# Last projection of a decoder trunk on one core: seven products for eight on 16 of its 22 feature blocks, set between the tiles of the projection before it

## The chip, the core and the metric

The program runs on one core of one Trainium2 chip. The core has a matrix engine (PE; its weight loads are shown apart as PEld), a vector engine (DVE), a scalar or activation engine (ACT), a general engine (POOL) and a queue engine that issues transfers (SP). Each engine takes its instructions in the order in which they were written and waits, where it must, for a signal of another engine or of a transfer. The metric is the device time of one execution in microseconds (us); lower is better. The time before is the median of three runs.

## The reference, cut to what matters

All arithmetic is in float32. The input `x` is (1, 512, 1024): 512 tokens of 1024 features, one layer. The part that the change touches is the channel mixer at the end and the last norm:

```
def conv_ffn(u, w_up, conv_w, conv_b, w_down):
    h = causal_dwconv(u @ w_up, conv_w, conv_b)
    a, v = h[..., :D_FF], h[..., D_FF:]
    return (jax.nn.silu(a) * v) @ w_down
...
        x = x + merged @ w_o[i]
        x = x + conv_ffn(rmsnorm(x, ln2_g[i]), ffn_w_up[i], ffn_conv_w[i], ffn_conv_b[i], ffn_w_down[i])
    return rmsnorm(x, final_g)
```

`D_FF` is 2816, that is 22 blocks of 128 features. `w_up` is 1024 x 5632, `w_down` is 2816 x 1024. The convolution has three taps along the tokens. Ahead of this stand a norm, a wide input projection, an attention, a pooling and a state-space branch, their gates, and the projection `w_o`.

## The kernel before

**Numbers.** Every matrix product is made of float32 operands split in a high and a low part (`wh`, `wl` for weights; `fh`, `fl` or `uh`, `ul` for the other side), each in a rounded format that the matrix engine takes. `mm3` (L230 is its matmul) adds three products, high by high, high by low and low by high, in one accumulator. The order matters below: the low part of the weights is only read in the last third of a group.

**Jobs.** The kernel is a list of jobs, each with a weight tile of 1 MB (some of 512 KB) and a body of matmuls. Before the body of job n is written, `prepare` writes three things: `low` of job n+1 (DVE: `wl = raw - wh`, L211), `cast` of job n+2 (ACT: `wh = raw`, L191, in two halves which are put off to the next two calls of `step`), and `fetch` of job n+3 (an SP transfer into `raw`, L179). There are two buffers for `raw`, three for `wh`, two for `wl`. `low` of job n+1 therefore waits until PE is done with job n-1, and `cast` until its transfer has landed. A job may have a `form` (its weights are a combination of loaded tiles, taken in place of `raw`), and a `then`, work on DVE that follows its `low`.

**Items.** Small work beside the matmuls (splitting a result, adding sums) is written as generators, in the list `running`. `step` is called once or twice a job; it writes the halves of a put-off `cast` first and then advances each running item by one piece.

**The up projection.** `up_jobs` makes 22 jobs. Jobs come in pairs: an even one holds two feature blocks of the half `a`, the odd one the same two blocks of `v`. Each has two chunks of 24 matmuls (128 x 128 by 512 columns). `up_evac` takes a chunk out of its accumulator `pu`: ACT scales it (L1162), DVE adds the two other taps (L1165 twice), then for `a` ACT applies silu (L1167), for `v` POOL multiplies with `a` (L1170). One `step` later the item `later` splits the block for the last projection (ACT L1177, DVE L1178).

**The last projection.** `down` and `blocks_of` follow after all up jobs. Output is kept in eight tiles `X1[tb, h]`, four token blocks by two halves of the 1024 columns, to which products are added. On the first `KS = 8` of the 22 blocks a two-by-two scheme with seven products instead of eight is used: blocks k and k+1 form the pair side, the column halves the other, and the token halves the third. A product is 24 matmuls (two token blocks i, four k blocks, three products of parts). The left sides are sums of the blocks (`sums_of`: four DVE operations of 256 columns, two ACT copies, two DVE differences for each pair of blocks), the right sides are combinations of quarters of `w_down` (`diff`, L333, 128 x 2048), where two quarters are loaded as `W`. The other 14 blocks are done plainly, by `blocks_of`, some in the same accumulators as two of the products. Because the scheme needs room, `put_x1` writes the eight `X1` tiles to DRAM after the fourth up job and `get_x1` brings them back after the last.

**The end.** `evac` of `blocks_of` adds the last accumulator, and for the second column half makes the final norm of that token block (`norm_late`) and sends it out. `tail=2` holds the last two jobs back and then runs them token block by token block.

**Buffers and queues.** Tiles of 128 x 512 come from one pool of `NBIG = 54`. `ypool`, tag `xs`, has two buffers of 128 x 4 x 512; before the change they hold `sh`, `sl` (parts of the sums) here. The order on PE, ACT, DVE and POOL is the order of writing; SP's order is set by a scheduler.

Of the kernel before, what the change touches and what calls it, by code (L numbers as in the profile page):

```python
# [10 lines left out]
F32 = mybir.dt.float32  # L11
# [5 lines left out]
P = 128  # L17
S = 512
# [10 lines left out]
SH = 16  # L29
DFF = 2816  # L30
KF = DFF // P
KS = 8
C_Q, C_K, C_V = 0, AW, 2 * AW
C_POOL = 3 * AW
C_Z = C_POOL + D
# [48 lines left out]
def trunk(ctx: ExitStack, tc, out, x, rel_bias, ln1_g, w_in, b_gate, w_a, pool_w, pool_scale, w_b,  # L84
# [26 lines left out]
    def MM(name):  # L111
        return psum.tile([P, S], F32, name=name, tag="mm")
# [978 lines left out]
    def get_x1():  # L1091
        back = upool.tile([P, KD, S], F32, name="x1b", tag="ul")
        for h in range(2):
            for tb in range(4):
                X1[tb, h] = back[:, 2 * tb + h, :]
                sp.dma_start(X1[tb, h], nxt["x1"][tb, h])

    def wo_jobs(pair, h):
        def evac(tb, ps):
            t = X1[tb, h]  # L1100
# [33 lines left out]


    ACTS = {}
    wide = []
    ff = {}

    def ff_cols():  # L1140
# [19 lines left out]
    def up_evac(m, ps):  # L1160
        t = HC[m] = T("hc")
        act.activation(t, ps, AF.Identity, bias=ff["c1"][:, ff["b"] + m:ff["b"] + m + 1], scale=fw(2, m))  # L1162
        for k in range(2):
            sh = 2 - k
            dve.scalar_tensor_tensor(t[:, sh:], ps[:, :S - sh], fw(k, m), t[:, sh:], OP.mult, OP.add)  # L1165
        if m < KF:
            act.activation(t, t, AF.Silu)  # L1167
            return
        a = HC[m - KF]
        pool.tensor_tensor(a, a, t, OP.mult)  # L1170

        def later():
            yield
            k = m - KF
            if k >= KS or k % 2:
                h, l = T("fh", F32R), T("fl", F32R)
                act.copy(h, a)  # L1177
                dve.tensor_sub(l, a, h.bitcast(F32))  # L1178
                ACTS[k] = (h, l)
                if k < KS:  # L1180
                    yield
                    for _ in sums_of(HC[k - 1], a, *(t[:, k // 2, :] for t in wide),
                                     lambda j, h, l: FS.__setitem__((j, k // 2), (h, l))):
                        yield
                return
            if k == 0:
                wide.extend(ypool.tile([P, 4, S], F32R, name=n, tag="xs") for n in ("sh", "sl"))
# [9 lines left out]
    def down():  # L1197

        n2 = KS // 2
        quarter = lambda two, h: w_down[:KS * P, h * S:(h + 1) * S].rearrange(
            "(k two p) c -> two p k c", two=2, p=P)[two]
        W, acc, rs, r3 = {}, {0: {}, 1: {}}, {}, {}

        def load_w():
            both = upool.tile([P, KD, S], F32, name="w3", tag="uh")
            for at in range(2):
                W[at] = both[:, 4 * at:4 * at + 4, :]
                sp.dma_start(W[at], quarter(at, 1))  # L1210
            get_x1()

        def product(ps, ws, parts, first, last):

            wh, wl = ws
            mm3(ps, lambda k: wh[:, k, :], lambda k: wl[:, k, :], lambda k: parts[k][0],
                lambda k: parts[k][1], range(n2), first, last, flip=True)

        def first_half(i):
            return [[t[:, i * P:(i + 1) * P] for t in FS[0, p]] for p in range(n2)]  # L1220

        def second_half(tb):
            return [[t[:, tb * P:(tb + 1) * P] for t in ACTS[2 * p + 1]] for p in range(n2)]

        def sums(j, i):
            return [[t[:, i * P:(i + 1) * P] for t in FS[j, p]] for p in range(n2)]

        def add(tb, h, what):
            dve.tensor_tensor(X1[tb, h], X1[tb, h], what, OP.add)

        def job(parts, use, form=None, ld=None):
            def body(ws):
                for i in range(2):
                    use(i, ws)
                    step()
            j = Job(parts, n2, S, body)
            j.form, j.load = form, ld
            return j


        def p2(i, ws):
            acc[0][i] = MM("pb")
            product(acc[0][i], ws, second_half(i), True, False)

        def p1(i, ws):
            ps = SM("p1")
            product(ps, ws, first_half(i), True, True)
            add(i, 0, ps)
            rs[i] = T("r1")
            act.copy(rs[i], ps)  # L1250
            if i:
                diff(W[0], W[1], W[0])

        def p5(i, ws):
            ps = SM("p5")
            product(ps, ws, sums(1, i), True, True)
            add(i, 1, ps)
            add(2 + i, 1, ps)

        def p7(i, ws):  # L1260
            ps = SM("p7")
            product(ps, ws, sums(3, i), True, True)
            r3[i] = T("r3")
            act.copy(r3[i], ps)

        def p6(i, ws):
            ps = SM("p6")
            product(ps, ws, sums(2, i), True, True)
            dve.tensor_tensor(rs[i], rs[i], ps, OP.add)
            dve.tensor_tensor(r3[i], r3[i], rs[i], OP.add)  # L1270

            def rest():
                yield
                add(2 + i, 0, r3[i])
                yield
                add(i, 1, rs[i])
                yield
                add(2 + i, 1, r3[i])
            running.append(rest())

        def p4(i, ws):
            product(acc[0][2 + i], ws, second_half(2 + i), False, True)
            add(2 + i, 0, acc[0][2 + i])
            running.append(early(2 + i))

        def p3(i, ws):
            acc[1][i] = SM("pb")
            product(acc[1][i], ws, sums(4, i), True, False)

        one = job([quarter(0, 0)], p1)  # L1290
        five = job([], p5, lambda: diff(one.raw, W[0], one.raw), lambda: None)
        def formed():
            diff(W[1], W[1], one.raw)
            return W[0]

        seven = job([], p7, formed, lambda: None)
        six = job([], p6, lambda: W[1], lambda: None)
        four = job([quarter(1, 0)], p4, lambda: diff(four.raw, four.raw, W[1]))
        plain = blocks_of(0, acc[0], (0, 1), (2, 3))

        yield Call(load_w)
        yield job([quarter(1, 0)], p2)
        yield next(plain)
        yield one
        yield five
        yield next(plain)
        yield seven
        yield next(plain)
        yield six
        yield from plain  # L1310
        yield four
        yield job([quarter(1, 1)], p3)
        yield from blocks_of(1, acc[1], (0, 1), ())

    def up_jobs():
        held = []
# [52 lines left out]
        yield  # L1369
        fin[tb] = norm_early(X1[tb, 0], fin["g"])  # L1370

    def blocks_of(h, acc, opened, keep):
# [12 lines left out]
        return jobs_b(lambda k0, k1: [wsrc(w_down, KS + k0, KS + k1, h * S, h * S + S)], S,  # L1385
                      lambda k, tb: ACTS[KS + k][0][:, tb * P:(tb + 1) * P],
                      lambda k, tb: ACTS[KS + k][1][:, tb * P:(tb + 1) * P], KF - KS, evac,
                      mk=(MM, SM)[h], tail=2 if h else 0, acc=acc, opened=opened, keep=keep)


    class Call:
# [3 lines left out]
    def program():  # L1395
# [34 lines left out]
        for pair in range(2):  # L1430
            for h in range(2):
                yield from wo_jobs(pair, h)
            if pair == 0:
                yield Call(ff_cols)
        for i, job in enumerate(up_jobs()):
# [220 lines left out]
```

## Time and profile before

| what | value |
|---|---|
| runs (us) | 1046.50, 1048.81, 1051.13; median 1048.81 |
| the profiled execution's own time | 1049.47 us |
| its span in the profile | 1047.4 us |
| granted PE clock over the span | 0.997 |
| matmuls | 5220 |
| up projection, full tiles | from about 696 to 925.5 us |
| last projection | from about 925.5 to 1040.5 us |
| what follows the last matmul | about 6.9 us |
| transfers over the span | 121.80 MB |

The span is what the profiler saw between the first and the last instruction; the execution's own time holds about 2 us more around it. Busy time of an engine is the sum of its instructions. "Idle before, releaser" says which signal ended an engine's wait. A matmul's record is longer than the distance to the next one, since they are pipelined; distances are read from the starts.

### The profile page before, as it was taken

To read this page: it belongs to the slowest core of one execution; us is meant where nothing else is said; L and a number is where in the kernel's file an instruction comes from. 1 tells how busy PE (TensorE), PEld (TensorE's weight loads), DVE (VectorE), ACT (ScalarE), POOL (GpSimd) and SP (SyncE) were. 2 spreads that over 40 slices of the span, in tenths; PEclk is the share of its full clock that TensorE was granted. 3 is DMA by queue.
4 is the path that set the end of the run, shared out by engine and by line. 5 is a ranking of instruction groups with operands and counts; after the bars stand their busy time and mean duration, and the time that the engine had idled before them with its cause. 6 is when DMAs were issued, how large, how long until landed. Compare 5 with 4: busy or idle time off the path is not lost.

```text
span 1047.4 us, 13090 instructions
## 1 busy us (share of the span) xinstructions
PE 1036.3 (99%) x5220; PEld 864.5 (83%) x5220; DVE 642.6 (61%) x865; ACT 467.6 (45%) x753; POOL 138.0 (13%) x118
## 2 busy tenths in 40 slices
PE   8999999999999999999999999999999999999997
PEld 8988877898888887787888888898888888878885
DVE  4563565774356647676658856766766566556645
ACT  5432555452474363557554324545444343433331
POOL 1680000000000001100143500001111111110110
PEclk9999999999999999999999999999999999999999
DMA  8445222127222363542252426643232322362322
GB/s 254 145 111 152 97 65 74 31 59 202 81 81 81 82 159 101 152 130 59 65 151 81 161 81 223 222 156 107 81 121 81 116 86 89 112 241 66 115 101 81
DMA packets 119787, 121.80 MB, mean 116 GB/s; under 512 B 5523, under 2 KB 101590, under 8 KB 119727
## 3 DMA queue, kind: packets, MB, share of 16 engines
q1 hardware_dynamic: 119135, 120.12, 37.1%
q8 instruction: 41, 0.67, 0.3%
q10 hardware_dynamic: 592, 0.86, 0.3%
q14 instruction: 19, 0.16, 0.0%
HBM read 115.07 MB, written 4.32 MB: 114 GB/s over the span
## 4 chain that ended last, share of the span: by engine, by line
PE 92%; DVE 3%; DMA 2%; ACT 2%; issue 0%; DVEq 0%; SPq 0%; ACTq 0%
PE pa L230 35%; PE pu L230 22%; PE pb L230 13%; PE pqk L230 9%; PE pa L1508 2%; PE p L230 2%; DVE wl L211 2%; PE ps L656 1%; PE po L695 1%; PE pt L683 1%; DMA raw<-in_ffn_w_up_dram 1%; PE ppw L230 1%; ACT wh L191 1%; PE py L955 1%; DMA raw<-in_w_o_dram 1%; PE pyo L961 1%
## 5 line engine op out<-in xcount | busy, mean ns | idle before, releaser
L211 DVE TENSOR_TENSOR wl<-raw,wh 128x2048 fp32r<-128x2048 f32 (+3 forms) x95 | 218.5, 2301 | 77.7 <-ACT wh L191 40.3
L191 ACT CAST wh<-raw 128x1024 fp32r<-128x1024 f32 (+3 forms) x188 | 189.6, 1026 | 67.4 <-DVE raw L333 21.1
L230 PE MATMUL pa<-uh,wh 128*128 128x512 f32 x384 | 98.7, 399 | 0.0
L1165 DVE SCALAR_TENSOR_TENSOR hc<-pu,fcol,hc 128x510 f32<-128x510 f32 x88 | 65.9, 748 | 50.8 <-ACT hc L1162 49.2
L230 PE MATMUL pa<-uh,wl 128*128 128x512 f32 x384 | 95.0, 389 | 0.0
L230 PE MATMUL pa<-ul,wh 128*128 128x512 f32 x384 | 94.9, 389 | 0.0
L230 PEld LDWEIGHTS pa<-ul,wh 128*128 128x128 f32 x384 | 72.1, 188 | 15.2
L230 PEld LDWEIGHTS pa<-uh,wl 128*128 128x128 f32 x384 | 72.0, 188 | 15.2 <-DVE wl L211 0.3
L230 PE MATMUL pu<-uh,wh 128*128 128x512 f32 (+1 forms) x352 | 83.7, 380 | 0.2 <-ACT uh L448 0.2
L230 PE MATMUL pu<-ul,wh 128*128 128x512 f32 (+1 forms) x352 | 83.5, 379 | 0.0
L230 PE MATMUL pu<-uh,wl 128*128 128x512 f32 (+1 forms) x352 | 83.5, 379 | 0.0
L230 PEld LDWEIGHTS pa<-uh,wh 128*128 128x128 f32 x384 | 70.2, 188 | 15.3 <-issue 1.0
L230 PEld LDWEIGHTS pu<-uh,wh 128*128 128x128 f32 x352 | 64.1, 188 | 12.8 <-ACT uh L448 0.4
L230 PEld LDWEIGHTS pu<-ul,wh 128*128 128x128 f32 x352 | 64.2, 188 | 12.5
L230 PEld LDWEIGHTS pu<-uh,wl 128*128 128x128 f32 x352 | 64.2, 188 | 12.5
L1162 ACT ACTIVATE hc<-pu,fcol,fcol 128x512 f32<-128x512 f32 x40 | 31.2, 780 | 75.5 <-PE pu L230 75.3
L1170 POOL TENSOR_TENSOR hc<-hc 128x512 f32<-128x512 f32 x22 | 31.5, 1432 | 223.6 <-DVE hc L1165 169.4
L934 POOL TENSOR_TENSOR xd<-xc,dec 128x512 f32<-128x512 f32 x6 | 6.4, 1065 | 360.1 <-DVE xc L925 334.5
L677 ACT ACTIVATE sb<-sb,nm 128x128 f32<-128x128 f32 (+1 forms) x72 | 30.1, 419 | 24.1 <-DVE nm L674 17.2
L1050 ACT ACTIVATE sg<-pa,col 128x512 f32<-128x512 f32 x24 | 16.5, 687 | 50.7 <-PE pa L230 50.6
L230 PE MATMUL pqk<-uh,wh 128*128 128x512 f32 x144 | 36.9, 394 | 0.0
L230 PE MATMUL pqk<-ul,wh 128*128 128x512 f32 x144 | 36.3, 389 | 0.0
(348 smaller groups left out, 1751.7 us busy)
## 6 DMA issues: line engine op xcount, KB each, us to landing
raw<-in_w_in_dram SPq DMA_DIRECT2D x25, 1024.0 KB
raw<-in_ffn_w_up_dram SPq DMA_DIRECT2D x22, 1024.0 KB
raw<-in_w_in_dram SPq DMA_DIRECT2D x20, 512.0 KB
raw<-in_ffn_w_down_dram SPq DMA_DIRECT2D x10, 1024.0 KB
raw<-in_w_o_dram SPq DMA_DIRECT2D x8, 1024.0 KB
raw<-in_w_b_dram SPq DMA_DIRECT2D x4, 1024.0 KB
al<-ad SPq DMA_DIRECT2D x16, 256.0 KB
raw<-in_w_c_dram SPq DMA_DIRECT2D x4, 1024.0 KB
```

The lines of the kernel that those rows point to most:

```text
L191: act.copy(job.high[:, :, o], job.raw[:, :, o])
L211: (eng or dve).tensor_tensor(l[:, :, o], job.raw[:, :, o], h[:, :, o].bitcast(F32), OP.subtract)
L230: pe.matmul(ps, l, r, start=first and n == 0, stop=last and n == total - 1)
L656: pe.matmul(pss[i][:, o:o + w * P], q[r, n * P:(n + 1) * P], k[r, kb * P:(kb + w) * P], start=True, stop=True)
L677: act.activation(sb[:, off:off + w * P], sb[:, off:off + w * P], AF.Exp, bias=nm[:, n, h:h + 1], accum_out=ls[:, n, h:h + 1])
L683: pe.transpose(pt[:, o:o + P], sb[:, o:o + P], eye)
L695: pe.matmul(po[DH * hh:DH * hh + DH, n * P:(n + 1) * P], V[g, kb + i][:, (2 * c + hh) * DH:(2 * c + hh + 1) * DH], probs[2 * c + hh, nb][: ...
L1050: act.activation(s, ps, AF.Sigmoid, bias=col[:, o:o + 1])
L1162: act.activation(t, ps, AF.Identity, bias=ff["c1"][:, ff["b"] + m:ff["b"] + m + 1], scale=fw(2, m))
L1165: dve.scalar_tensor_tensor(t[:, sh:], ps[:, :S - sh], fw(k, m), t[:, sh:], OP.mult, OP.add)
L1170: pool.tensor_tensor(a, a, t, OP.mult)
L1508: pe.matmul(first[2 * n + j][:, lo:hi], a[:, k, j * P:(j + 1) * P], b[:, k, lo:hi], start=a is wh and b is uh and k == 0, stop=a is wl and ...
```

## The change

`KS` goes from 8 to 16, in two groups of eight blocks. `down_group(base)` writes the seven products of a group as jobs of their own, and `program` sets them between the up jobs: the table `AT` says after which up job each product stands (22 stands for "after the first plain job of the last projection"). Six blocks are left for the plain scheme (`down_jobs`). No product shares an accumulator with plain blocks any more: every product goes through an accumulator `pd`, and its result is added to the `X1` tiles on DVE, or kept in a tile `r1`, `r2`, `r5`, `r7` by ACT and added later. The seven additions of a group's last steps are written one per step. `X1` stays on chip, and `put_x1` and `get_x1` are gone; the `xs` buffers now hold the two quarters `W` of a group. In `later` the four DVE sums are made in the same step as the high part of the odd block, one step sooner than before.

The order of jobs is then: up 0 to 9, three, up 10, seven, up 11, one, up 12, five, up 13, six, up 14, two, up 15, four (A22), up 16, up 17, three', seven', up 18, one', up 19, five', up 20, six', up 21, two', first plain job, four', the other plain jobs. (A prime marks the second group; three is the product of the fourth sum with `W[1]`, four the one of `A22`.)

```
-KS = 8
+KS = 16
...
-    def put_x1():
-        nxt["x1"] = dram.tile([4, 2, P, S], F32, name="x1d")
-        for tb, h in X1:
-            sp.dma_start(nxt["x1"][tb, h], X1[tb, h])
...
             if k >= KS or k % 2:
                 h, l = T("fh", F32R), T("fl", F32R)
                 act.copy(h, a)
+                it = iter(())
+                if k < KS:
+                    it = sums_of(HC[k - 1], a, T("sah", F32R), T("sal", F32R),
+                                 lambda j, h, l: FS.__setitem__((j, k // 2), (h, l)))
+                    next(it)
                 dve.tensor_sub(l, a, h.bitcast(F32))
                 ACTS[k] = (h, l)
-                if k < KS:
+                yield
+                for _ in it:
                     yield
...
+        def load():
+            for two in range(2):
+                W.append(ypool.tile([P, 4, S], F32, name="w3", tag="xs"))
+                sp.dma_start(W[two], quarter(two, 1))
...
+        def p1(i, ps):
+            keep(r1, "r1")(i, ps)
             add(i, 0, ps)
...
+        def p5(i, ps):
+            keep(r5, "r5")(i, ps)
+            dve.tensor_tensor(r2[i], r2[i], ps, OP.add)
+
+        def p6(i, ps):
+            dve.tensor_tensor(r1[i], r1[i], ps, OP.add)
 
             def rest():
                 yield
+                dve.tensor_tensor(r7[i], r7[i], r1[i], OP.add)
+                for tb, h, r in ((i, 1, r1), (2 + i, 0, r7), (i, 1, r2), (2 + i, 1, r7), (2 + i, 1, r5)):
+                    yield
+                    add(tb, h, r[i])
             running.append(rest())
...
+        def then1():
+            diff(W[0], W[0], one.raw)
+            dve.tensor_tensor(W[1], W[1], one.raw, OP.add)
+
+        one = job("A11", quarter(0, 0), None, p1)
+        two = job("A12", quarter(1, 0), None, lambda i, ps: add(i, 0, ps))
+        three = job(4, None, lambda: W[1], keep(r2, "r2"))
+        three.then = lambda: diff(W[1], W[1], W[0])
+        one.then = then1
+        two.then = lambda: diff(two.raw, two.raw, W[1])
+        return load, [[three], [job(3, None, lambda: W[1], keep(r7, "r7"))], [one],
+                      [job(1, None, lambda: W[0], p5)], [job(2, None, lambda: W[1], p6)],
+                      [two], [job("A22", None, lambda: two.raw, lambda i, ps: add(2 + i, 0, ps))]]
...
         for i, job in enumerate(up_jobs()):
             yield job
-            if i == 3:
-                yield Call(put_x1)
+            for load, ats in zip(loads, AT):
+                if i == ats[0] - 3:
+                    yield Call(load)
+            yield from between.get(i, ())
         yield Call(lambda: fin.setdefault("g", grow(final_g)))
-        yield Call(finish)
-        yield from down()
+        plain = down_jobs(0)
+        yield next(plain)
+        yield from between.get(2 * (KF // 2), ())
+        yield from plain
+        yield from down_jobs(1)
...
+AT = ((9, 10, 11, 12, 13, 14, 15), (17, 17, 18, 19, 20, 21, 22))
```

More of the change, by code (lines that the diff above doesn't have):

```diff
@@ L1136, in trunk @@
     ACTS = {}
-    wide = []
     ff = {}
@@ L1195, in trunk, with down_group @@
     FS = {}
-    def down():
-        n2 = KS // 2
-        quarter = lambda two, h: w_down[:KS * P, h * S:(h + 1) * S].rearrange(
+    def down_group(base):
+        quarter = lambda two, h: w_down[base * P:(base + 8) * P, h * S:(h + 1) * S].rearrange(
             "(k two p) c -> two p k c", two=2, p=P)[two]
[L1204 to L1226, printed above, removed]
@@ new lines, in down_group, with side @@
+        W, r1, r2, r5, r7 = [], {}, {}, {}, {}
+        def side(j):
+            ks = range(base, base + 8, 2)
+            if j == "A11":
+                return [FS[0, k // 2] for k in ks]
+            if j == "A12":
+                return [[t[:, LO] for t in ACTS[k + 1]] for k in ks]
+            if j == "A22":
+                return [[t[:, HI] for t in ACTS[k + 1]] for k in ks]
+            return [FS[j, k // 2] for k in ks]
+        def load():
+            for two in range(2):
+                W.append(ypool.tile([P, 4, S], F32, name="w3", tag="xs"))
+                sp.dma_start(W[two], quarter(two, 1))
@@ L1228, in add, with job @@
         def add(tb, h, what):
             dve.tensor_tensor(X1[tb, h], X1[tb, h], what, OP.add)
-        def job(parts, use, form=None, ld=None):
+        def job(j, raw, form, use):
             def body(ws):
+                wh, wl = ws
+                parts = side(j)
                 for i in range(2):
-                    use(i, ws)
-                    step()
[L1236 to L1243, printed above, removed]
@@ L1266, in p6 @@
[L1266 to L1270, printed above, removed]
+                    ps = SM("pd")
+                    o = slice(i * P, (i + 1) * P)
+                    mm3(ps, lambda k: wh[:, k, :], lambda k: wl[:, k, :],
+                        lambda k: parts[k][0][:, o], lambda k: parts[k][1][:, o], range(4), flip=True)
+                    use(i, ps)
@@ new lines, in body, with keep, use @@
+                    step()
+            new = Job([raw] if raw is not None else [], 4, S, body)
+            new.form = form
+            if raw is None:
+                new.load = lambda: None
+            return new
+        def keep(r, name):
+            def use(i, ps):
+                r[i] = T(name)
+                act.copy(r[i], ps)
+            return use
+        def p1(i, ps):
+            keep(r1, "r1")(i, ps)
+            add(i, 0, ps)
+        def p5(i, ps):
+            keep(r5, "r5")(i, ps)
+            dve.tensor_tensor(r2[i], r2[i], ps, OP.add)
@@ L1286, in p3 @@
[L1286 to L1313, printed above, removed]
+                dve.tensor_tensor(r7[i], r7[i], r1[i], OP.add)
+                for tb, h, r in ((i, 1, r1), (2 + i, 0, r7), (i, 1, r2), (2 + i, 1, r7), (2 + i, 1, r5)):
+                    yield
+                    add(tb, h, r[i])
@@ L1434, in program @@
                 yield Call(ff_cols)
+        loads, groups = zip(*(down_group(base) for base in range(0, KS, 8)))
+        between = {}
+        for group, ats in zip(groups, AT):
+            for jobs_, at in zip(group, ats):
+                between.setdefault(at, []).extend(jobs_)
         for i, job in enumerate(up_jobs()):
             yield job
-            if i == 3:
-                yield Call(put_x1)
+            for load, ats in zip(loads, AT):
+                if i == ats[0] - 3:
+                    yield Call(load)
+            yield from between.get(i, ())
         yield Call(lambda: fin.setdefault("g", grow(final_g)))
-        yield Call(finish)
-        yield from down()
+        plain = down_jobs(0)
[3 more added lines that the diff above has]
+        yield from down_jobs(1)
     jobs = list(program())
```

41 lines of the change are left out of this document (2 added, 39 removed).

## The prediction

> **What bounds the kernel now.** I read the shares of the engines first, then the chain of work that ended last, in order of time, then busy time by stretch, then DVE's instructions at places like those where the new products will stand.
>
> ```profile
> PE 1036.3 (99%) x5220; PEld 864.5 (83%) x5220; DVE 642.6 (61%) x865; ACT 467.6 (45%) x753; POOL 138.0 (13%) x118
> ```
>
> ```profile
> 925.45 5.45 PE pb L230 x24
> ...
> 930.94 2.25 DVE wl L211
> ...
> 933.23 9.36 PE pb L230 x40
> 942.59 10.88 PE p L230 x48
> ...
> 986.11 54.41 PE pb L230 x240
> ```
>
> PE is busy 99% of the span, and in the chain (start, length, what) it is followed by itself: from 696 to 1040.5 us only one link is another engine's, a `low` at 930.94. 240 matmuls take 54.41 us, so one costs 0.2267 us wherever nothing is late, and a product or chunk of 24 takes 5.44 us, an up job 10.88 us.
>
> ```profile
> 706.90:925.06 218.16, 218.16 (x967) 180.76 (x966) 138.43 (x146) 96.12 (x130) 29.91 (x21) 1.00 0.30 99
> 925.06:986.11 61.05, 60.52 (x267) 49.83 (x266) 33.67 (x24) 19.75 (x24) 1.59 (x1) 1.00 0.42 149
> 986.11:1040.49 54.38, 54.38 (x240) 44.71 (x239) 31.60 (x46) 16.08 (x29) 7.98 (x4) 1.00 0.26 89
> 1040.49:1047.40 6.91, 0.02 (x1) 0.00 (x0) 3.08 (x8) 0.93 (x3) 0.00 (x0) 0.76 0.41 151
> ```
>
> Columns: length, then busy us of PE, PEld, DVE, ACT and POOL, clock, share and GB/s of the transfers. In the up stage PE has no gap in 218 us, DVE is busy 63%, ACT 44%, transfers 30%, the clock is 1.00. So time is made by the number of matmuls, and any other work is free until it makes PE wait.
>
> ```profile
> 926.30 1.54 DVE L1165 SCALAR_TENSOR_TENSOR hc<-pu,fcol,hc 128x510 f32<-128x510 f32 x2 [3.62 <-ACT hc L1162]
> 927.76 0.69 DVE L1178 TENSOR_TENSOR fl<-hc,fh 128x512 fp32r<-128x512 f32 x1
> 930.28 0.69 DVE L1178 TENSOR_TENSOR fl<-hc,fh 128x512 fp32r<-128x512 f32 x1 [1.83 <-ACT fh L1177]
> 930.89 4.49 DVE L211 TENSOR_TENSOR wl<-raw,wh 128x2048 fp32r<-128x2048 f32 x2
> ...
> 933.23 0.96 PE L230 MATMUL pb<-wl,fh 128*128 128x512 f32 x3 [0.53 <-DVE wl L211]
> ```
>
> This is how PE comes to wait: at the seam of the last up job (PE left it at 925.06) DVE must first finish that chunk, then two splits, then `low` of the next job but one. It ends 8.1 us after the seam; PE wanted it after 24 + 8 matmuls, 7.25 us. The wait was 0.53 us, the only one of its kind.
>
> ```profile
> 817.50 1.54 DVE L1165 SCALAR_TENSOR_TENSOR hc<-pu,fcol,hc 128x510 f32<-128x510 f32 x2 [3.81 <-ACT hc L1162]
> 818.96 0.69 DVE L1178 TENSOR_TENSOR fl<-hc,fh 128x512 fp32r<-128x512 f32 x1
> 819.57 3.38 DVE L211 TENSOR_TENSOR wl<-raw,wh 128x2048 fp32r<-128x2048 f32 x1
> ```
>
> The same seam between two up jobs. The `low` took 3.38 us where it takes 2.29 us elsewhere (809.96, with POOL idle): POOL's product ran from 819.18 to 820.79.
>
> **The change part by part.**
>
> *Matmuls.* 22 blocks done plainly would be 528 matmuls; each group of seven products saves 24. The instruction list of the changed kernel has 5196 for 5220. Minus 24 x 0.2267 = **5.44 us**. A page of the Trainium skill speaks against reading PE as full: Perfetto Trace Analysis, "Identifying the Most-Contended Engine", says that matmul busy time is a bad measure and weight-load busy the good one. By it, 24 loads of 188 ns would go, an estimate of 4.5 us. The distance of the starts decides here, 0.2267 us at no idle, so I keep 5.44.
>
> *DVE work*, counted from the two instruction lists, by rows of before: sums for four more block pairs, 16 x 0.42 = 6.7 and 8 more low parts x 0.68 = 5.4; four more weight combinations x 2.29 = 9.2; three more `low` x 2.29 = 6.9; 28 more additions of 512 columns x 0.69 = 19.3. Together 47.5 us. ACT gets 6 half casts x 1.04, 12 `r` copies x 0.59, 8 sum copies x 0.62, less 0.8: about 17.5 us. POOL's work stays. On the path this costs nothing while PE covers it, and the cover is thinner than before: from up 9 to the seam before two', DVE's rows sum to 159.8 us where PE needs 13 x 10.88 + 12 x 5.44 = 206.7 us, 77% for the 63% above.
>
> *The seams.* What counts is whether `low` ends in time at each product. With T the end of an up job, the rows above give: taps done at T+2.8, one split at T+3.4, `low` at T+6.7 with POOL's collision. After an even job silu and half a cast stand in between; there 809.96 + 2.29 is 6.9 us after the job's end (805.38). PE wants it at T + 5.44 + 3.63 = 9.07 where an up job follows the product (16 matmuls stand ahead of the first `wl`), and at T+7.25 where a product or plain job follows. So:
> - three, seven, one, five and their second-group likes (an up job next): 6.7 or 6.9 against 9.07, cost 0.
> - three' to seven' (two products in a row): 6.7 against 7.25, cost 0; a second collision of 1.1 would make it 0.6.
> - six, up 14, two, up 15, four is the heaviest stretch: DVE's rows are 6.7, 11.7, 6.4, 8.0 and 6.0, 38.9 us against 38.1 us of PE. Step by step, with starts 0.61 us apart for a row of 0.69 as in the traces (818.96 to 819.57): after six begins, taps 2.8, split 3.4, `low` of up 14 6.7, then one addition, four sums, a split and two additions, 10.6, that is 5.2 into up 14. There `low` of two 7.4, its combination 9.6, first taps 11.1, low parts 12.2, two additions 13.4; ACT, held by these taps, does silu, half a cast and the second chunk's scaling by 13.5; second taps 15.0, 4.1 into two. ACT's silu and the other half cast end 5.9 into two, DVE's two additions 5.3; `low` of up 15 ends at 8.1, and PE wants it at 9.07. Cost 0; bounds 0 and 2.2 (two more collisions of 1.1, less the slack, twice).
> - two' to the first plain job: taps 2.8, two additions held by POOL's product to 5.1, one split 5.7, `low` 8.0 against 7.25: cost **0.7**. The old wait of **0.53** at this seam goes. Bounds 0 and 1.8.
>
> The Trainium skill has a rule for the collision: SBUF — State Buffer, "SBUF: two separate sides", says that a DVE operation with two SBUF inputs and a GpSimd operation lock one shared port pair for a whole instruction and the later one blocks. The 3.38 us agrees. It speaks against the change, whose 28 additions mostly stand right where POOL multiplies; had each of the 13 seams lost a whole POOL product of 1.3 us, the sum would still lie within the slack at most of them.
>
> *Transfers.* `X1` no longer goes out and back (16 transfers, 4.2 MB), and 2 MB of `w_down` less are loaded. PE waited for none of these, so no gain. The quarters `W` of the first group are now issued early: in the new SP order they stand between the loads of `w_a` and `w_c`, waiting for the `xs` buffers, which DVE leaves at about 569 and 586 us; the loads behind them went out at 575.5 and later, and the first `w_c` job begins at 592.9. Cover: about 7 us; cost 0, and up to one 1 MB landing (6.4 us in the chain at 687.01), less that cover, if it is gone. A product with no load of its own lets the next load go out sooner; only two holds its `raw` until four's `low`, which puts the load of up 16 at 2.7 us into up 15, landing about 6.4 us later, some 5 us before its `low`.
>
> *Buffers.* In the new kernel each of the 54 tiles is taken again only after readers that PE has passed in the order of writing; the closest is a copy in the last step of six, behind that product's own matmuls. Cost 0.
>
> *The end.* The last two jobs, 18 matmuls a token block, and the norm are as before: 6.91 us.
>
> **Sum.** 1049.47 - 5.44 - 0.53 + 0.7 = 1044.2 us for the profiled execution, which lies 0.66 us above the median of the runs shown; so **1043.5 us** as a median, 5.3 us or 0.5% less. Its own bounds are 1042.6 (no wait left) and 1045.0.
>
> **Rivals.**
> *Short waits at many seams.* DVE takes instructions in order, so a late one is carried to the next seam; one collision more (1.1 us) at each of two to four tight seams gives back 1 to 4.4 us: 1044.6 to 1048. For it: 77% load, and 102% in the stretch of six. Against it: a PE wait at only one of the seams shown, and 9.07 against 6.9 at most.
> *Slower: DVE becomes the bound between up 9 and two'.* From 790 to 925 us DVE waited 28.3 us for the taps' first step, 13.3 for splits and 10.7 for casts, 4.2 us for each up job. If these waits all stay under the new load: 159.8 + 13 x 4.2 + 7 collisions x 1.1 = 222.1 us where PE needs 206.7, so 15.4 - 5.4 = 10 us slower, **1058.8 us**. It decides from the point where over four fifths of them stay (44.6 of 54.6 us). For it: a DVE that waits for ACT's silu and cast after an even job cannot use that time. Against it: it waits mostly because it is early, and a DVE behind its work finds ACT done.
> *A load comes late* (first `w_c`, or up 16): 1 to 5 us on top, 1044.5 to 1048.5.
> That the products are not fewer is ruled out by the count of 5196.
>
> **How the numbers follow.** 0.5% is 5.2 us, about what a measurement of this kernel can tell from no change. Forecast 0.66: its sum lies just past that line, and as either seam wait can be absent, I put 0.50 to faster and 0.16 to within. Short waits 0.15, all within. DVE bound 0.16, of which 0.15 slower. Late load 0.03, of which 0.02 slower. Faster 0.50, same 0.33, slower 0.17. The range 1041.5 to 1049.5 takes the forecast and the short waits, with 1 us of scatter below, and leaves the DVE-bound case out.
>
> **What would show it.** 5196 matmuls; PE busy about 1031 us and its gaps from 696 us to the last matmul under 1.5 us in all, one of them 0.3 to 1 us before `wl` of the first plain job; DVE near 690 us busy, its share from up 9 on at 75% or more; `wl` of three' and of up 15 ended before PE asks. It is wrong if PE shows gaps of 1 us or more at several products, each ended by `low` on DVE, or if the time between two up jobs grows by more than 5.44 us for a product, or if PE waits for a transfer ahead of `w_c` or up 16.

## The result and the profile after

| what | before | after |
|---|---|---|
| median (us), range | 1048.84, 1046.50 to 1051.13 (6 runs) | 1043.96, 1042.02 to 1044.99 (6 runs) |
| ratio to before, 95% interval | | 0.9954, 0.9943 to 0.9965 |
| profiled execution, its span | 1049.47, 1047.4 | 1044.67, 1042.3 |
| granted PE clock over the span | 0.997 | 0.997 |
| matmuls | 5220 | 5196 |
| transfers over the span | 121.80 MB | 115.51 MB |

The kernel became 4.9 us faster, 0.46%: just short of the line of 0.5% that the prediction drew, with an interval that lies on both sides of it. The forecast was 1043.5 us.

The engines' shares on the page of the changed kernel:

```profile
PE 1030.8 (99%) x5196; PEld 859.8 (82%) x5196; DVE 689.9 (66%) x924; ACT 483.7 (46%) x779; POOL 136.1 (13%) x118
```

PE lost 5.5 us of busy time and DVE gained 47.3. The chain of work that ended last, in order of time (start, length, what), at the first product and at the last jobs:

```profile
795.05 1.59 PE pd L230 x7
...
796.67 4.15 PE pd L230 x17
800.83 10.88 PE pu L230 x48
811.71 5.44 PE pd L230 x24
...
996.52 2.21 DVE wl L211
...
998.78 9.37 PE pb L230 x40
```

An up job is 10.88 us and a product 5.44 us, in turn, from 800.83 us on; none of these products stretches the job before or after it. The first product, from 795.05 to 800.83 us, took 5.78 us. Only at the seam near 996 us does the chain leave PE for long.

Busy time by stretch (length, then PE, PEld, DVE, ACT, POOL, clock, share and GB/s of the transfers): up jobs before the first product, up jobs and products, what follows the wait at the first plain job.

```profile
696.46:795.05 98.59, 98.59 (x482) 83.62 (x481) 72.63 (x81) 45.51 (x63) 11.95 (x9) 1.00 0.27 88
795.05:998.78 203.73, 203.39 (x897) 167.75 (x896) 156.89 (x154) 96.08 (x126) 19.74 (x14) 1.00 0.27 88
998.78:1035.36 36.58, 36.56 (x160) 29.95 (x160) 27.14 (x48) 10.91 (x24) 6.02 (x4) 1.00 0.26 88
```

In the middle stretch DVE is busy 156.89 of 203.73 us, 77%. In the stretch that the prediction had summed, from up 9 to the seam before two', it is 157.94 of 206.67 us, 76% for the 77% forecast. PE's matmuls have only one gap that ends with a signal. That gap in the timeline of DVE, and then of PE, which answers the seam near 930 us of before:

```profile
992.08 1.54 DVE L1152 SCALAR_TENSOR_TENSOR hc<-pu,fcol,hc 128x510 f32<-128x510 f32 x2 [0.73 <-ACT hc L1149]
993.53 2.38 DVE L1207 TENSOR_TENSOR x<-x,r 128x512 f32<-128x512 f32 x2
995.84 0.68 DVE L1170 TENSOR_TENSOR fl<-hc,fh 128x512 fp32r<-128x512 f32 x1
996.44 2.28 DVE L211 TENSOR_TENSOR wl<-raw,wh 128x2048 fp32r<-128x2048 f32 x1
...
998.78 1.19 PE L230 MATMUL pb<-wl,fh 128*128 128x512 f32 x4 [0.30 <-DVE wl L211]
```

Two additions took 2.38 us where two others take 1.28, then the split and `low` follow, and PE waits 0.30 us for it.

A second loss shows only in the weight loads. These are lines of the timelines of DVE, PE and PEld at the first product:

```profile
794.83 1.79 DVE L328 TENSOR_TENSOR sbl<-sb,sbh 128x512 fp32r<-128x512 f32 x1
795.79 1.38 PE L230 MATMUL pd<-wh,sbl 128*128 128x512 f32 x4
796.67 0.19 PEld L230 LDWEIGHTS pd<-wh,sbl 128*128 128x128 f32 x1 [0.46 <-DVE sbl L328]
797.01 1.09 PE L230 MATMUL pd<-wl,sbh 128*128 128x512 f32 x4
```

The low part of a sum took 1.79 us where it takes 0.69 in the run without POOL's product, since POOL multiplies from 794.46 to 796.06 us. One weight load waits 0.46 us for it, and the next four matmuls start 1.22 us after these four and not 0.91, as elsewhere: 0.31 us lost.

**Where the time came from.** I compare the length from the first full up tile to the end of the last matmul, since the start of this stretch moves by 1 us and more from one execution to the next with the same work ahead of it: 694.6 to 696.7 us in all profiles but one. The start is taken 0.80 us ahead of the tile's second eight matmuls. The chain has it there too where the tile's first matmul does not wait; where it waits for ACT, as in the kernel before, the chain starts 0.27 us earlier, and that is left out. The stretch was 696.30 to 1040.52, 344.22 us, before, and is 696.46 to 1035.36, 338.90 us, after: 5.32 us less. 24 matmuls at 0.2267 us are 5.44, and the rest is small waits, which grew a little. Before, PE lost 0.53 us and 0.29 behind that wait, 0.82 in all; the changed kernel loses 0.30 and 0.30 behind it, and 0.31 at the first product, 0.91. A version without these (the last experiment) takes 337.97 us, 0.93 less than the changed kernel.

### The profile page after: what moved, and what is told of

The parts are those of the page before. It is cut to its first block, busy times and chain, and to the rows that moved or that the text cites. A ratio compares the mean times of both kernels' runs of the same rounds, so it can differ in the third digit from the quotient of the medians.

```text
span 1042.3 us, 13073 instructions
## 1 busy us (share of the span) xinstructions
PE 1030.8 (99%) x5196; PEld 859.8 (82%) x5196; DVE 689.9 (66%) x924; ACT 483.7 (46%) x779; POOL 136.1 (13%) x118
## 2 busy tenths in 40 slices
DMA packets 116427, 115.51 MB, mean 111 GB/s; under 512 B 5235, under 2 KB 101302, under 8 KB 116367
## 4 chain that ended last, share of the span: by engine, by line
PE 94%; DVE 3%; DMA 1%; ACT 1%; issue 1%; POOL 0%; ACTq 0%; DVEq 0%; POOLq 0%
PE pa L230 32%; PE pu L230 22%; PE pb L230 12%; PE pqk L230 9%; PE pd L230 7%; PE pa L1469 2%; PE ps L656 1%; PE pu L1279 1%; PE po L695 1%; PE pt L683 1%; PE ppw L230 1%; PE py L955 1%; DVE wl L211 1%; PE pyo L961 1%; DMA wb<-wd 1%; DMA eye<-in_c_eye_dram 1%
## 5 line engine op out<-in xcount | busy, mean ns | idle before, releaser
L211 DVE TENSOR_TENSOR wl<-raw,wh 128x2048 fp32r<-128x2048 f32 (+3 forms) x92 | 214.5, 2332 | 52.1 <-ACT wh L191 43.9
L191 ACT CAST wh<-raw 128x1024 fp32r<-128x1024 f32 (+3 forms) x182 | 183.6, 1026 | 42.4 <-DMA raw<-in_w_in_dram 15.2
L230 PEld LDWEIGHTS pa<-ul,wh 128*128 128x128 f32 x384 | 72.1, 188 | 15.2
L1157 POOL TENSOR_TENSOR hc<-hc 128x512 f32<-128x512 f32 x22 | 31.7, 1441 | 288.4 <-DVE hc L1152 253.6
```

What stands on the lines that cost most here:

```text
L191: act.copy(job.high[:, :, o], job.raw[:, :, o])
L211: (eng or dve).tensor_tensor(l[:, :, o], job.raw[:, :, o], h[:, :, o].bitcast(F32), OP.subtract)
L230: pe.matmul(ps, l, r, start=first and n == 0, stop=last and n == total - 1)
```

## The experiments

Diffs are against the changed kernel. Each comparison is with the kernel before, run on the same chip; "the stage" is the length defined above.

**One group only.** All edits stay (items a step sooner, additions one per step, `X1` on chip, the products of the first group between up jobs), but the scheme covers 8 blocks.

```
-KS = 16
+KS = 8
```

> The changed kernel with the scheme on one group of eight blocks (KS = 8), 14 blocks plain; X1 still stays on chip, items and additions as in the changed kernel. Theory (time is the number of matmuls): 24 matmuls more than the changed kernel, 24 x 0.2267 = 5.44 us, so 1043.96 + 5.4 = 1049.4 us, the time before; PE without waits of a microsecond. Rival (the gain came from X1 staying on chip, from accumulators of their own and from the seam): the time stays at 1044 to 1046 us, as all of that is kept.

Measured: 1048.52 us (10 runs), ratio 1.0000 (0.9990 to 1.0009); stage 343.7 us. The chain from after the first group to the last matmul:

```profile
897.97 65.28 PE pu L230 x288
963.25 76.17 PE pb L230 x336
```

Six up jobs and fourteen blocks in a row, without a wait, and the time is that of before. The stage is 0.5 us shorter: the old wait with what follows it is gone, and the 0.31 us at the first product is there. So next to nothing but the count of matmuls pays: `X1` on chip, fewer transfers, products as jobs of their own and the old wait are together worth less than the times can tell. With that 0.31 us taken off, the stage is 5.44 us longer than without any wait (337.99 in the last experiment): the 24 matmuls.

**Items a step later.** The sums of a pair are made one step later, as before the change.

```
-                it = iter(())
-                if k < KS:
-                    it = sums_of(HC[k - 1], a, ...)
-                    next(it)
                 dve.tensor_sub(l, a, h.bitcast(F32))
                 ACTS[k] = (h, l)
-                yield
-                for _ in it:
+                if k < KS:
                     yield
+                    for _ in sums_of(HC[k - 1], a, ...):
+                        yield
```

> The changed kernel with the sums made one step later, as before the change. Theory: the low parts of the sums are then written after the seam of up 9, behind the taps, at 4.2 to 5.3 us, where PE asks for the last of them 1.6 us into product three: one wait of 2.6 to 3.7 us there, none at three' (two more steps lie between), so 1046.5 to 1047.7 us. Rival (the step is free, as DVE has room): 1044 us.

Measured: 1048.73 us (10 runs), ratio 1.0001 (0.9991 to 1.0010). The first line is from PE's timeline, the others from busy time by stretch:

```profile
797.93 0.50 PE L230 MATMUL pd<-wh,sbl 128*128 128x512 f32 x1 [3.12 <-DVE sbl L328]
```

```profile
798.00:800.00 2.00, 2.00 (x7) 1.58 (x8) 2.00 (x2) 0.19 (x1) 0.00 (x0) 0.68 0.00 0
800.00:802.00 2.00, 2.00 (x6) 1.62 (x5) 0.53 (x2) 1.85 (x3) 0.00 (x0) 0.50 0.18 25
```

PE waits 3.12 us for the low part of a sum in the very first product, as expected, and then the granted clock is 0.68 and 0.50: 17 matmuls take 5.77 us where they need 3.85. So this version loses 3.1 + 1.9 = 5.0 us there, where the changed kernel loses 0.3; that is 4.7 of the 5.1 us by which the stage (344.0 us) is longer. With its sums a step later the change would have brought nothing at all.

**All additions at once.** The five additions at the end of a group, which each of a product's two token blocks has, are made in one step.

```
                 for tb, h, r in ((i, 1, r1), (2 + i, 0, r7), (i, 1, r2), (2 + i, 1, r7), (2 + i, 1, r5)):
-                    yield
                     add(tb, h, r[i])
```

> The changed kernel with the additions after product six written in one step instead of one per step; the same number of them. Theory: they stand in the heaviest stretch ahead of low of up 15 (about 12 us into two, wanted at 9.07: 2.8 us of wait) and of the first plain job (9.4 us into two', wanted at 7.25: 2.2 us), so about 4.5 us on top, 1048.5 us, between 1046 and 1050. Rival (only the total of DVE's work counts, and that is the same): 1044 us.

Measured: 1055.88 us (4 runs), ratio 1.0072 (1.0055 to 1.0089). PE's timeline, then the chain behind the first wait, then the clock behind the second:

```profile
889.64 3.54 PE L230 MATMUL pu<-uh,wl 128*128 128x512 f32 x8 [4.03 <-DVE wl L211]
...
1007.74 1.21 PE L230 MATMUL pb<-wl,fh 128*128 128x512 f32 x4 [3.90 <-DVE wl L211]
```

```profile
889.64 9.02 PE pu L230 x32
```

```profile
1010.00:1012.00 2.00, 2.00 (x6) 1.60 (x5) 1.69 (x1) 0.00 (x0) 0.00 (x0) 0.50 0.36 137
```

The two waits are at up 15 and at the first plain job, the two seams named, but 4.03 and 3.90 us long for the 2.8 and 2.2 expected, and each is followed by half clock: 32 matmuls in 9.02 us for 7.25, and 40 in 10.98 for 9.07. 7.9 us of waits and 3.7 us of slow clock, less the 0.6 us that the changed kernel loses at the second place, make the 11.0 us by which the stage (349.9 us) is longer. The total of DVE's work is the same as in the changed kernel. So the place of the additions in the queue is worth 12 us here, at the same total.

**Products in a row.** All seven products of a group stand behind up 9, and behind up 17.

```
-AT = ((9, 10, 11, 12, 13, 14, 15), (17, 17, 18, 19, 20, 21, 22))
+AT = ((9, 9, 9, 9, 9, 9, 9), (17, 17, 17, 17, 17, 17, 17))
```

> The changed kernel with the seven products of a group one behind the other, after up 9 and after up 17, instead of one after each up job. Theory (a seam must be covered by the up job beside it): DVE has about 41 us of work for 38 us of PE in each row, and chains of combination, cast and low within 5.44 us; 3 to 6 us lost in each row, about 1052 us, between 1047 and 1058. Rival (77% load is low enough wherever the products stand): 1044 us.

Measured: 1044.34 us (5 runs), ratio 0.9955 (0.9940 to 0.9970); stage 339.3 us. My theory fell: there is one wait of 0.32 us, and each row's first product has the 0.3 us that the changed kernel loses at its first. Busy time in the two rows of products (columns as above):

```profile
795.05:833.15 38.10, 37.74 (x165) 30.59 (x164) 36.73 (x34) 19.59 (x26) 2.21 (x2) 1.00 0.35 111
921.03:959.13 38.10, 38.07 (x169) 31.21 (x168) 35.21 (x28) 18.93 (x24) 2.63 (x2) 1.00 0.17 55
```

DVE is busy 36.73 of 38.10 us, 96%, and PE has gaps of 0.36 us. I had counted 41 us of work; the taps and splits in the row are only those of the last up job before it, and additions that are late trail into the up jobs behind (the last at 847 us). So standing singly between the tiles of the mixer is not what makes the change pay: rows within the up stage do as well. Products behind all up jobs were not tried.

**More work on DVE behind each product**, two, four and eight additions of the products' own form, on a tile that nothing reads.

```
+                spin = T("spin")
+                for _ in range(4):
+                    dve.tensor_tensor(spin, X1[0, 0], X1[0, 0], OP.add)
```

> Four more additions of the form of the products' own (128x512, 0.61 us from start to start in the profile of the changed kernel) behind each of the 14 products, on a tile that nothing reads: VectorE gets 34 us more in the stage, nothing else changes. Theory (VectorE's queue runs behind each product and has some 1.6 us of cover left before the work that TensorE wants next: the weights of up 15 end 7.44 us into their product and are wanted at 9.07): the weights of up 15 come 0.8 us late, those of the first plain job 2.1 us late for the 0.3 of now, so 1046.5 us (1045.5 to 1048.5; 1.8 more if one wait passes 3 us, since the clock then falls to half for a while). Rival (the cover is wide, since VectorE's total of 66% leaves a third of the time free): 1044, no new wait.

> Eight such additions behind each product, 68 us more of VectorE's work in the stage. Theory (queue behind each product): waits of TensorE of some 3.2 us at up 15, 2.4 at up 16 and 4.2 at the first plain job, and 1.8 us of half clock behind each that passes 3 us: about 1057 us (1051 to 1061). Rival by the total load alone (219 us of VectorE's work for 206.7 of TensorE's, shared out over the stage): 1056, but with waits spread over most of the jobs between the first product and the last instead of standing at two or three seams. Rival (the cover is wide): 1044.

Measured: with four 1054.28 us (4 runs), ratio 1.0048 (1.0034 to 1.0063); with eight 1089.94 us (4 runs), 1.0385 (1.0368 to 1.0401). PE's waits after 790 us with four (engine, releaser, then us in total, times, longest), and busy time from the first product to the first plain job:

```profile
PE pb L230 <- DVE wl L211: 3.3, 2, 2.2
PE pu L230 <- DVE wl L211: 3.0, 3, 1.4
PE pd L230 <- DVE wl L211: 1.7, 1, 1.7
```

```profile
795.29:1006.90 211.61, 204.56 (x896) 167.44 (x895) 187.85 (x202) 95.44 (x126) 19.46 (x14) 1.00 0.26 85
```

The two waits that I named came, 1.21 us at up 15 and 2.24 us at the first plain job. But there are four more (1.39 at up 16, 1.75 in seven', 0.45 at up 19 and 1.06 among the last plain jobs): a queue that is late at one seam starts late into the next. The four additions also took 2.78 us where four of the products' own, 0.60 us apart, take 2.4; all four write the same tile, which may be why. 8.1 us of waits and 0.29 us after each, less the one that was there, make the 9.3 us of the stage. With eight, in the same stretch:

```profile
794.40:1038.07 243.67, 215.31 (x896) 170.78 (x895) 220.17 (x250) 95.08 (x126) 19.06 (x14) 0.97 0.23 74
```

DVE is busy 89% of the stretch with four and 90% with eight. It does not come nearer to full: with eight, 19.5 of its 23.5 us without work are waits for ACT. PE then waits at most seams, 31.7 us in 17 waits, as the rival by load said of the place. The three waits of the theory are among them, 2.28 us at up 15, 1.86 at up 16 and 6.84 at the first plain job. The rival's load was right too, 219 us forecast and 220.17 measured; its price was not, 45 us and not 12, because it took a DVE that can be busy all the time, and left out the half clock that follows some of the waits.

> Two more additions behind each of the 14 products; the four of the earlier run took 0.70 us each, not 0.61, so two are 1.4 us. Theory A (cover at each seam): the weights of up 15 end at 7.44 + 1.4 = 8.84 us of the 9.07 they have, no wait; the first plain job waits 0.3 + 1.4 = 1.7 us; nothing else: 1045.4 us (1044.5 to 1046.5). Theory B (VectorE can be busy some 90% of the stretch from the first product to the first plain job, as in both runs with four and eight, and TensorE waits only from there on): 156.9 + 12 x 1.4 = 173.7 us of 203.7 are 85%, no new wait: 1044.0. Theory C (the loss is in proportion to the additions, half of what four cost): waits at four to six places and 1049.

Measured: 1044.73 us (5 runs), ratio 0.9962 (0.9947 to 0.9978); stage 340.3 us, DVE 84% of the stretch. PE's waits:

```profile
PE pb L230 <- DVE wl L211: 0.8, 1, 0.8
PE pd L230 <- DVE wl L211: 0.3, 1, 0.3
```

No wait at up 15, as theory A had it; 0.79 us at the first plain job instead of 1.7, and 0.30 in seven', which A did not have. Theory B, no new wait, is not right either, though its time, 1044.0 us, is as near as A's 1045.4. Worked out afterwards: DVE waited 0.73 us for ACT ahead of its last taps there (the first line of the seam above), and takes that time up first. Theory C is out, since the loss is not in proportion: 1.4, 9.3 and 46 us of stage for two, four and eight. For additions at this place the loss becomes large between 84 and 89% of the stretch, not at 100%.

**POOL's multiplication on DVE.**

```
-        pool.tensor_tensor(a, a, t, OP.mult)
+        dve.tensor_tensor(a, a, t, OP.mult)
```

> The multiplication that GpSimd does in each up job goes to VectorE, so that GpSimd has nothing left in this stage that VectorE's instructions could run into; VectorE gets one more operation of about 0.69 us per up job. Theory (the 3.38 us that some of the weights' 128x2048 operations take for 2.29, and the two late additions at the first plain job, are GpSimd's collisions): no weights of 3.4 us are left in the stage, the wait of 0.3 us at the first plain job goes, the time stays at 1043.5 to 1044.5. Rival (the long ones have another cause, so VectorE only gets more work): the 3.4 us remain, TensorE waits 0.5 to 1 us more at up 15 and the first plain job, 1045 to 1046.

Measured: 1042.97 us (6 runs), ratio 0.9935 (0.9921 to 0.9949); stage 338.2 us, no gap of PE and no loss at the first product. The same `low` in DVE's timeline of the changed kernel, then of this one:

```profile
863.30 3.38 DVE L211 TENSOR_TENSOR wl<-raw,wh 128x2048 fp32r<-128x2048 f32 x1
```

```profile
863.75 2.28 DVE L211 TENSOR_TENSOR wl<-raw,wh 128x2048 fp32r<-128x2048 f32 x1
```

In the changed kernel POOL multiplies from 863.22 to 864.53 us, under that `low`. No `low` of the stage takes over 2.33 us now. DVE got 22 operations of 0.69 us more, 15.2 us, and its busy time fell from 689.9 to 686.5: the collisions had cost it 18.6 us, 0.85 for each product of POOL. The work is cheaper on the loaded engine than beside it.

**The sixth product of the second group one job later**, two' behind the first plain job.

```
-AT = (..., (17, 17, 18, 19, 20, 21, 22))
+AT = (..., (17, 17, 18, 19, 20, 22, 22))
```

> The sixth product of the second group (the one that stood between the first and the second plain job's up part as seen from the seam) is placed one job later, beside the seventh: its items then do not stand ahead of the first plain job's weights. Theory: the wait of 0.3 us at the first plain job's products goes, the time stays within the scatter, 1043.4 (1042.5 to 1044.5). Rival (two products in a row leave VectorE no plain job to catch up in): a new wait of 1 to 3 us in or behind the seventh product, 1045 to 1048.

Measured: 1043.06 us (5 runs), ratio 0.9942 (0.9928 to 0.9956); stage 338.3 us. The wait at the first plain job is gone as expected; the 0.6 us of stage are the wait and what followed it, and are within the scatter of the times.

**Both together**, and once more beside the changed kernel.

> GpSimd's multiplication on VectorE and the sixth product of the second group one job later, together: each alone took the last wait of the stage away and gave some 338.2 us from the first full up tile to the last product's end for the 338.9 of the changed kernel. Theory (what is left is TensorE's own work): nothing more to win, 338.2 us and 1043.0 (1042 to 1044), no wait. Rival (the longer up jobs on VectorE now meet two short jobs in a row): a wait of 1 to 2 us at the plain jobs, 1044.5 to 1046.

> The changed kernel as it is, beside the next run on the same chip: 1044 us, 338.9 us from the first full up tile to the last product's end, one wait of 0.3 us at the first plain job.

> The kernel with GpSimd's multiplication on VectorE and the sixth product one job later once more, beside the changed kernel. Theory (the two win the 0.9 us of the stage, 338.0 for 338.9, and the early start of the stage in its first profile, 692.98 us, was scatter): 1043.1 us, the stage's start again between 694 and 697 us. Rival (the early start belongs to the kernel): start near 693 us, 1041 us.

Measured: both 1041.23 us (5 runs), ratio 0.9936 (0.9922 to 0.9949), stage 337.97 us from 692.98; again 1042.17 (6 runs), 0.9933 (0.9916 to 0.9950), stage 337.99 us from 695.50; the changed kernel beside it 1043.73 (6 runs), 0.9951 (0.9936 to 0.9966), stage 338.96. The end of the stage in the chain of the second run of both:

```profile
989.96 10.88 PE pb L230 x48
1000.84 10.88 PE pd L230 x48
1011.72 21.77 PE pb L230 x96
```

PE follows itself to the last matmul. The early start of the first profile did not come again, so it does not belong to the kernel. The stage is 0.97 us shorter in the trace; the times, 1.6 us apart, agree, but the intervals overlap. This is the best version that I ran, and no wait is left to win in this stage.

## Why the prediction was right, point by point

- *Matmuls.* 24 fewer at 0.2267 us, 5.44 us, was the gain. The run with one group shows that no other part has one: 24 matmuls more, and the time of before to 0.1%. The rule of the Trainium skill that was weighed (Perfetto Trace Analysis, "Identifying the Most-Contended Engine") gave an estimate of 4.5 us by weight loads; stage against stage it is 5.32, and 5.41 with the waits of both sides (0.82 and 0.91) taken off, so the distance of the matmuls decided.
- *DVE's work.* 47.5 us forecast, 689.9 - 642.6 = 47.3 measured, 77% of its stretch forecast and 76% measured. That it is covered was right but for the 0.9 us of waits, and it was close: the run with two additions, 15 us more in this stretch, shows the first new wait.
- *The seam at up 15.* `low` forecast at 8.1 us after two begins, wanted at 9.07. In the timeline it starts at 882.14 and takes 2.29 us, so it ends 7.60 us after two's first matmul at 876.83 (7.44 after two's link in the chain, which the expectations used). The slack is some 1.5 us, and the runs with two and four additions, without and with a wait there, bear it out.
- *The first plain job.* Wait forecast 0.7, measured 0.30 (0.3 again in the second profile). Counted from 990.84, 0.23 us before the product's first matmul as in the prediction, `low` ended at 7.9 us for the 8.0 forecast; the term was mis-sized by when PE asks, 7.25 us forecast and 7.6 in the trace (998.78 less the wait of 0.30). The lines of before held this already: with `low` ending 8.1 us after the seam, asking at 7.25 would have made a wait of 0.85 us, and it was 0.53. Left out, here and for the old wait, is the 0.3 us that PE loses behind a wait.
- *The first product.* The seams were judged by `low` alone, at a cost of 0 for three. There the low part of the sum came last, with POOL's collision under it, and cost 0.31 us.
- *Transfers, buffers, the end.* No wait for a transfer, 6.94 us after the last matmul for 6.91.
- *The sum.* 1044.2 us for the profiled execution, measured 1044.67; 1043.5 as a median, measured 1043.96. Old and new waits were forecast to add 0.17 us in all and added some 0.1, but by other terms: the new wait was taken too long (0.7 for 0.30), and the 0.3 us behind each wait and the 0.31 at the first product were missing. That these cancel is luck. The 0.5 us above the forecast stand ahead of the stage (0.2) and outside the profiled span (0.3). That the change would pass the line of 0.5% was given a chance of one half, and it ended 0.04 percent points short.
- *The rivals.* Short waits at many seams and a DVE that becomes the bound did not come in this kernel. Both are real, though: two steps that the change takes beside the products keep them away, the sums a step sooner (5 us) and the additions one per step (12 us). The prediction named no price for their absence; in the expectations, at some 3 and 4.5 us, both were mis-sized, by the clock that falls after the wait and, for the additions, by the waits' length. The point from which DVE decides was put at 44.6 us of its waits for ACT staying. In this kernel 47.5 us of them stayed in that stretch and DVE did not decide, because its rows with all collisions came to 157.9 us and not to 159.8 + 7.7: with that the point is 206.7 + 5.4 - 157.9 = 54.2 of the 54.6 us. Waits do stay under more load (DVE stops at 90% with eight additions).
- *POOL's collisions.* The rule quoted from SBUF — State Buffer, "SBUF: two separate sides", of a shared port pair held for a whole instruction, is what the run without POOL's product shows: `low` 2.28 us for 3.38. It did not decide, because the slack took most of it; what it cost, at the first product and at the first plain job, is the 0.7 us by which the stage is shorter without it.

## What to carry to other kernels

Where one engine is busy 99%, only its own instructions count, and the question for work that is put beside them is not how busy the other engine is but how late its queue is at the next seam: the same DVE total gave 5 us faster, no change or 7 us slower, by the step in which it was written. Work out the slack at each seam from the timeline, for every operand that PE reads and not for `low` alone. In this kernel a stretch of 200 us bore a load of some 84% with little loss, and a row of 38 us one of 96%. Try an operation that collides on the loaded engine itself. Where waits come near 2 us, add the price of the clock.

## What the hardware showed unexpectedly

A wait of PE costs more than its length. After waits of 0.3 to 2.24 us in the kernels above, the next 40 matmuls took 9.36 to 9.40 us for 9.07, 0.3 us more, at a clock of 1.00. After waits of 3.12, 3.90 and 4.03 us the granted clock was 0.50 for about 3.4 us, and the matmuls behind took 1.8 to 1.9 us more. Between these the length alone does not decide. Both lines are of PE's timeline with eight additions:

```profile
839.48 2.11 PE L230 MATMUL pu<-uh,wl 128*128 128x512 f32 x8 [2.44 <-DVE wl L211]
...
974.40 3.62 PE L230 MATMUL pu<-uh,wh 128*128 128x512 f32 x8 [2.05 <-ACT wh L191]
```

Eight matmuls after 2.44 us run at full pace and after 2.05 us at half. The Trainium skill (TensorE: Matmul & The Clock Gate, "What's actually happening") has the clock fall after an idle window of about 3.4 us that runs freely, and rise after 3.4 us of work. The length of the slow phase agrees; the fall after waits of 2.05 and 3.12 us doesn't, as they are shorter than such a window.

The kept profiles show what else decides. With eight additions the clock fell at 851.73, 899.51, 950.71, 974.60 and 1036.04 us, and these times are 14, 15, 7 and 18 times 3.413 us apart. So I cut the time from there into stretches of 3.413 us. Two of them, each with the one behind it (columns as above):

```profile
848.31:851.73 3.42, 1.63 (x8) 1.03 (x7) 3.38 (x4) 0.00 (x0) 0.00 (x0) 1.00 0.05 4
851.73:855.14 3.41, 3.41 (x10) 2.64 (x9) 2.24 (x4) 2.24 (x3) 0.00 (x0) 0.50 0.87 302
...
885.86:889.27 3.41, 1.66 (x7) 1.38 (x8) 3.38 (x2) 0.00 (x0) 0.00 (x0) 1.00 0.01 2
889.27:892.69 3.42, 2.30 (x11) 1.54 (x9) 3.38 (x6) 1.27 (x2) 0.00 (x0) 1.00 0.46 111
```

PE was busy 1.63 us of a stretch, and the clock was half in the next; with 1.66 us it stayed full. The same cut holds in all fourteen profiles, from 30 us to the last matmul: each of the eight falls follows a stretch with 1.63 us of PE or less, and no stretch with 1.66 us or more is followed by one. So a wait halved the clock where about 1.8 us of it lay in one such stretch: the 2.44 us were divided over two of them, 1.03 and 1.41 us, and the 2.05 us lay in one. This was read from the traces afterwards; no run was made to test it.
